# Nineteen gate and up pairs of a transformer layer made from seven block products each

## The chip, the core and the metric

The kernel runs on one core of a Trainium2 chip. TensorE (PE) multiplies, VectorE (DVE), ScalarE (ACT) and GpSimd (POOL) work on tiles, and DMAs are issued from the queues of SyncE (SP) and ScalarE. The metric is device time in microseconds of one execution. The kernel is float32: a product of two float32 matrices is made as three products of "high" and "low" parts (fp32r), and accumulated in PSUM.

## The reference

Two layers work on 512 latent and 256 context tokens of width 1024. What matters here is the second half of a layer, the gated feed-forward with a centred convolution of width 3 over the tokens:

```
def conv_ffn(h, w_up, conv_w, conv_b, w_down):
    u = h @ w_up                                  # 1024 -> 2 x 2816
    u = conv over tokens, width 3, per channel (u, conv_w) + conv_b
    a, bv = jnp.split(u, 2, axis=-1)
    return (jax.nn.silu(a) * bv) @ w_down
...
x = x + gt2 * conv_ffn(h2, ffn_up[l], ffn_conv_w[l], ffn_conv_b[l], ffn_down[l])
if with_ctx:
    ctx = ctx + cgt2 * conv_ffn(hc2, ...)
```

In layer 0 all 768 tokens go through it, in layer 1 only the 512 latent ones. The modulation vectors (`gt2` and others) are products of a conditioning vector with `ada_w`.

## The kernel before

Features lie on partitions, tokens in the columns. The normed input `h` is held as `hh` (high part) and `hl` (low part), eight blocks k of 128 features by 768 tokens. The 2816 hidden channels are 22 tiles of 128, and each tile has a gate half and an up half. One `Job` makes one half of one tile: it loads two raw weight tiles of 128x512 (`load`, on SP), splits each into `wh` (a copy by ACT, line 455) and `wl` (a subtraction, line 457, on DVE, on POOL for a few jobs), and multiplies in `chunk` (line 473): for every k three passes, hh with wh, hl with wh, hh with wl, over 512 and then 256 columns (`by_seg`). The result lies in a two-bank PSUM tile `pg`, of which there are two, so that job n+2 needs the bank of job n.

The evacuation `ev_up` makes the convolution: the centre tap by ACT (line 1484, scale and bias), the two side taps by DVE straight from PSUM (lines 1487, 1489), each for 512 and 256 columns. The gate half gets a SiLU (ACT, line 1496); after the up half the two are multiplied (DVE, line 1508) and split into `ah` (ACT) and `al` (DVE, line 576), the input of the down projection.

The 22 tiles come in groups (`GROUPS`) of 8, 7 and 7. After a group, eight down jobs multiply its 8 or 7 activation tiles with `dn` weights and add gate times result to `x` in SBUF (`residual`, line 1325, DVE).

The order is written out by program: `flow` walks through the list of jobs and issues for each, at fixed chunks, the loads and splits of the next two jobs and the evacuation of the last. Beside them run generators of side work: `beat` adds the nominal time of each matmul pass times `rate` to a budget, and a step of side work is issued for every unit of it. In the feed-forward of layer 0 the side work is `ada_rows`, the modulation vectors: per step a weight tile from DRAM and one or two DVE products with accumulation (line 656), with a small addition (line 659) in the second half. `rate` is 0.12 in the up jobs and 0.5 from the second down job on. Instructions of an engine run in the order in which they were issued.

## Time and profile before

| | |
|---|---|
| time, median of 3 runs | 2338.53 us (2338.52 to 2339.19) |
| the profiled execution: time, span | 2338.43 us, 2336.7 us |
| PE busy | 2296.9 us, 98% of the span, 13610 matmuls |
| DVE busy | 1417.8 us, 61% |
| ACT busy | 930.3 us, 40% |
| POOL busy | 299.9 us, 13% |
| chain that ended last | PE 86%, DVE 6%, ACT 3% |

"Busy" counts the time in which at least one instruction of the engine runs; matmuls overlap, so their mean length is larger than the time from one start to the next. The granted clock is a share of 2.4 GHz. The chain that ended last is followed back from the last instruction, at each step to what released it.

The feed-forward of layer 0 lies between about 822 and 1380 us: the first pair follows the norm chunk by chunk, and from 847.3 on jobs follow one another.

### The profile page before, as it was taken

Reading aid. Unit: us, or ns where it says so; the run is one execution under the profiler, and the core shown is the slowest. Engines: PE = TensorE matmul, PEld = TensorE weight load, DVE = VectorE, ACT = ScalarE, POOL = GpSimd, SP = SyncE. Lnnn points to the kernel's source line nnn. Section 1 sums busy time; section 2 is a strip of 40 time slices with the busy share of each in tenths; the row PEclk is TensorE's granted clock in tenths of the full one; section 3 lists DMA queues with packets and bytes.
Section 4 is the critical chain, followed back from the end, with each engine's and each line's share of the span. In section 5 each row is a group of like instructions: output and inputs, shape, how many; then the busy total and the mean of one; then the engine's idle time right before and its main releaser. Section 6 shows DMA issues by size and latency. Waiting matters only on the chain.

```text
span 2336.7 us, 35302 instructions
## 1 busy us (share of the span) xinstructions
PE 2296.9 (98%) x13610; PEld 1987.8 (85%) x13610; DVE 1417.8 (61%) x2856; ACT 930.3 (40%) x1623; POOL 299.9 (13%) x256
## 2 busy tenths in 40 slices
PE   8999999999999999999999999999999999999999
PEld 6888988888888888888888887989888888888887
DVE  5756485523878478766686656546753555646564
ACT  5655533322222253313313346554443335434342
POOL 0211163000111020000000024113500211000000
PEclk9999999999999999999999999999999999999999
DMA  7111112322454333462362322111233333332333
GB/s 269 50 41 39 53 51 95 94 65 88 144 169 137 104 100 108 136 185 95 103 195 91 104 86 69 46 46 51 95 114 116 95 108 105 99 99 92 99 99 100
DMA packets 132840, 235.79 MB, mean 101 GB/s; under 512 B 14460, under 2 KB 25980, under 8 KB 132544
## 3 DMA queue, kind: packets, MB, share of 16 engines
q1 hardware_dynamic: 123200, 223.57, 30.2%
q10 hardware_dynamic: 9472, 9.96, 1.2%
q8 instruction: 107, 1.75, 0.3%
q14 instruction: 61, 0.50, 0.1%
HBM read 220.37 MB, written 13.11 MB: 100 GB/s over the span
## 4 chain that ended last, share of the span: by engine, by line
PE 86%; DVE 6%; ACT 3%; issue 2%; POOL 1%; DMA 1%; POOLq 0%; ACTq 0%; SPq 0%; DVEq 0%
PE pg L473 72%; PE pg L485 6%; PE pm L912 2%; PE pm L901 1%; PE pm L1093 1%; PE ps L849 1%; PE pm L1115 1%; PE ps L848 1%; PE pm L1116 1%; DVE P L894 0%; DVE qs L1056 0%; PE pm L1282 0%; DVE Sg L1106 0%; DVE P L860 0%; DVE wl L457 0%
## 5 line engine op out<-in xcount | busy, mean ns | idle before, releaser
L473 PE MATMUL pg<-hh,wh 128*128 128x512 f32 (+1 forms) x2384 | 816.3, 354 | 7.4 <-ACT hh L1672 2.1
L473 PE MATMUL pg<-hl,wh 128*128 128x512 f32 (+1 forms) x2384 | 814.8, 354 | 0.8 <-POOL hl L307 0.7
L473 PE MATMUL pg<-hh,wl 128*128 128x512 f32 (+1 forms) x2384 | 812.5, 353 | 1.0 <-DVE wl L457 0.7
L457 DVE TENSOR_TENSOR wl<-raw,wh 128x512 fp32r<-128x512 f32 x500 | 356.5, 722 | 340.9 <-ACT wh L455 297.4
L473 PEld LDWEIGHTS pg<-hh,wh 128*128 128x128 f32 x2384 | 439.5, 190 | 72.8 <-issue 4.5
L473 PEld LDWEIGHTS pg<-hl,wh 128*128 128x128 f32 x2384 | 439.7, 190 | 61.3 <-DVE hl L1673 1.6
L473 PEld LDWEIGHTS pg<-hh,wl 128*128 128x128 f32 x2384 | 439.2, 189 | 61.0 <-issue 1.3
L455 ACT ACTIVATE wh<-raw 128x512 fp32r<-128x512 f32 (+1 forms) x556 | 334.4, 618 | 326.2 <-PE pg L473 163.2
L656 DVE SCALAR_TENSOR_TENSOR junk<-adr,crow 128x512 f32<-128x512 f32 x256 | 193.7, 757 | 11.2 <-DMA adr<-adv 7.5
L457 POOL TENSOR_TENSOR wl<-raw,wh 128x512 fp32r<-128x512 f32 x56 | 75.9, 1370 | 762.1 <-PE pg L473 549.7
L473 PE MATMUL pg<-al,wh 128*128 128x512 f32 (+1 forms) x500 | 171.5, 357 | 1.4 <-DVE al L576 1.4
L473 PE MATMUL pg<-ah,wh 128*128 128x512 f32 (+1 forms) x500 | 170.8, 356 | 0.0
L473 PE MATMUL pg<-ah,wl 128*128 128x512 f32 (+1 forms) x500 | 170.5, 355 | 0.0
L1313 POOL TENSOR_TENSOR M<-M,sg 128x768 f32<-128x768 f32 (+1 forms) x30 | 58.4, 1945 | 532.9 <-DVE sg L1311 532.9
L1301 ACT ACTIVATE sg<-pg 128x768 f32<-128x768 f32 (+1 forms) x48 | 33.7, 703 | 215.3 <-PE pg L473 215.3
L473 PEld LDWEIGHTS pg<-al,wh 128*128 128x128 f32 x500 | 91.4, 189 | 15.6 <-DVE al L576 2.3
L1487 DVE SCALAR_TENSOR_TENSOR acc<-pg,sml,acc 128x511 f32<-128x511 f32 (+1 forms) x129 | 84.8, 658 | 31.8 <-ACT acc L1484 31.4
L473 PEld LDWEIGHTS pg<-ah,wl 128*128 128x128 f32 x500 | 91.5, 189 | 13.8
L473 PEld LDWEIGHTS pg<-ah,wh 128*128 128x128 f32 x500 | 91.2, 189 | 13.9 <-ACT ah L575 0.4
L1325 DVE SCALAR_TENSOR_TENSOR X<-pg,mod,X 128x512 f32<-128x512 f32 (+1 forms) x72 | 45.7, 659 | 86.7 <-PE pg L473 86.7
L1484 ACT ACTIVATE acc<-pg,sml 128x768 f32<-128x768 f32 (+1 forms) x86 | 75.6, 879 | 38.2 <-PE pg L473 37.7
L1489 DVE SCALAR_TENSOR_TENSOR acc<-pg,sml,acc 128x511 f32<-128x511 f32 (+1 forms) x129 | 85.3, 661 | 4.6
(282 smaller groups left out, 3099.1 us busy)
## 6 DMA issues: line engine op xcount, KB each, us to landing
raw<-win SPq DMA_DIRECT2D x184, 256.0 KB, 2.9
raw<-up SPq DMA_DIRECT2D x176, 256.0 KB, 2.9
...
```

The costliest lines, as they stand in the source:

```text
L455: nc.scalar.activation(out=hi, in_=raw, func=AF.Copy)
L457: eng.tensor_tensor(out=lo, in0=raw, in1=hi.bitcast(F32), op=ALU.subtract)
L473: nc.tensor.matmul(job.ps[0:m, lo:hi], job.w[k // 4][a][:, k % 4, :], job.h(k, b)[:, lo:hi], start=(k == 0 and n == 0), stop=(k == job.nk ...
L485: nc.tensor.matmul(job.ps[:, 256 * t:256 * t + 256], job.h(k, b)[:, o:o + 128], job.w[k // 2][a][:, k % 2, :], start=(k == 0 and n == 0 an ...
L656: nc.vector.scalar_tensor_tensor(out=junk, in0=raw, scalar=1.0, in1=cr[v], op0=ALU.mult, op1=ALU.mult, accum_out=acc)
L912: nc.tensor.matmul(po[64 * kv:64 * kv + 64, 0:256], self.att["Va"][:, kb, 64 * kv:64 * kv + 64], PT[b][:, 256 * kv:256 * kv + 256], start= ...
L1301: nc.scalar.activation(out=sgs[d][:, 0:n], in_=ps[:, 0:n], func=AF.Tanh, scale=0.5)
L1313: eng.tensor_tensor(out=m, in0=m, in1=sg[:, 0:n], op=ALU.add)
L1325: nc.vector.scalar_tensor_tensor(out=X(d)[:, lo:hi], in0=ps[:, lo:hi], scalar=gate(d, int(lo >= TL)), in1=xin[:, lo:hi], op0=ALU.mult, op1 ...
L1484: nc.scalar.activation(out=acc[:, 0:nq], in_=ps[:, 0:nq], func=AF.Identity, scale=cw(1), bias=self.s("cb", 44 * l + u))
L1487: nc.vector.scalar_tensor_tensor(out=acc[:, lo + 1:hi], in0=ps[:, lo:hi - 1], scalar=cw(0), in1=acc[:, lo + 1:hi], op0=ALU.mult, op1=ALU.add)
L1489: nc.vector.scalar_tensor_tensor(out=acc[:, lo:hi - 1], in0=ps[:, lo + 1:hi], scalar=cw(2), in1=acc[:, lo:hi - 1], op0=ALU.mult, op1=ALU.add)
```

## The change

In layer 0 the first three tiles (`PLAIN`) stay as they are. The other 19 pairs go through the new class `Seven`. The weights of gate and up of a tile are a matrix of 2 x 2 blocks (gate or up, by features 0 to 511 or 512 to 1023: r11, r12, r21, r22), the input is one of 2 x 2 blocks (the same halves of the features, by tokens 0 to 383 or 384 to 767). Winograd's form of Strassen's scheme makes the product of the two from seven products of blocks, of 128 channels x 512 features x 384 tokens, with sums before and after.

- The sums of input blocks are made once (`blocks_begin`, `blocks_end`): 24 additions on POOL and 20 instructions on DVE of 384 columns, with splits, issued beside the plain tiles 1 and 2. They fill the tiles `T` (slots 1, 3 and 0), and one block `u` overwrites the right half of hh and hl, blocks 0 to 3.
- The sums of weight blocks are made for every pair on POOL (`weights`): four additions, and five of the seven low parts; the other two low parts are DVE's. There are three pairs of weight tiles, used in turn.
- The sums of products are made on DVE (`sums`), seven instructions of 384 columns from PSUM into SBUF tiles `g` and `u`. The taps then read those tiles. The stages 7 to 12 of a pair run beside the products of the next one, and after the last pair of a group in `tail`, beside the down jobs.
- Since slots 1 and 3 are taken, `x` is kept in DRAM (`xm`): the out projection stores it, each down job loads its tile (`xback`, two ahead) and stores it again (on ACT's queue), and only the last group's results stay in SBUF.
- The groups of layer 0 become 6, 6, 5 and 5 tiles. In the first two down jobs of a group the last chunk of the first comes after all but the last chunk of the second.
- The side work is paced anew: 0.04 in the pairs, 0.56 in the down jobs from the first on, and the products for `gt2` are put ahead, behind those of `sc2`.

```
-GROUPS = [(0, 8), (8, 15), (15, 22)]
+GROUPS = [[(0, 6), (6, 12), (12, 17), (17, 22)], [(0, 8), (8, 15), (15, 22)]]
+PLAIN = 3
+HT = TA // 2
...
+class Seven:
+    ORDER = ["p1", "p6", "p7", "p5", "p2", "p4", "p3"]
...
+    def parts(self, g, raw, eng):
...
+        hi, lo = self.q[g % 3]
+        p.split(self.r[raw], hi, lo, eng)
...
+    def weights(self, i, s):
...
+        if s == -3:
+            add("y", "r11", "r21")
+        elif s == -2:
+            self.parts(g, "r11", nc.vector)
+            add("x", "y", "r22")
+        elif s == -1:
+            self.parts(g + 1, "x", nc.gpsimd)
+        elif s == 0:
+            add("r21", "r21", "r22")
+            self.parts(g + 2, "y", nc.gpsimd)
+        elif s == 1:
+            self.parts(g + 3, "r21", nc.gpsimd)
+            add("x", "x", "r12")
+        elif s == 2:
+            self.parts(g + 4, "r12", nc.vector)
+        elif s == 3:
+            self.parts(g + 5, "r22", nc.gpsimd)
+        elif s == 4:
+            self.parts(g + 6, "x", nc.gpsimd)
...
+        if s == 1:
+            d["g"] = p.tP("g")
+            nc.scalar.activation(out=d["g"][:, left], in_=d["a"], func=AF.Copy)
+        elif s == 2:
+            d["V"] = p.t3("V")
+            tt(out=d["V"][:, left], in0=d["b"], in1=d["g"][:, left], op=V)
+        elif s == 3:
+            tt(out=d["V"][:, right], in0=d["c"], in1=d["V"][:, left], op=ALU.add)
...
+        elif s == 6:
+            tt(out=d["u"][:, left], in0=d["b"], in1=d["V"][:, right], op=ALU.add)
+            d["au"] = centre(d["u"], t + NFF)
+            tap(d["au"], d["u"], t + NFF, 0)
+        elif s == 7:
+            tt(out=d["g"][:, right], in0=d["c"], in1=d["g"][:, right], op=ALU.add)
+            d["ag"] = centre(d["g"], t)
+            tap(d["au"], d["u"], t + NFF, 2)
+        elif s == 8:
+            tap(d["ag"], d["g"], t, 0)
+        elif s == 10:
+            tap(d["ag"], d["g"], t, 2)
+            nc.scalar.activation(out=d["ag"], in_=d["ag"], func=AF.Silu)
+        elif s == 11:
+            tt(out=d["ag"], in0=d["ag"], in1=d["au"], op=ALU.mult)
+        elif s == 12:
+            self.end(t, d["ag"])
...
+            for s, name in enumerate(self.ORDER):
+                hi, lo = self.q[(7 * i + s) % 3]
+                T = self.blocks[name]
+                for m, (a, b) in enumerate(((hi, 0), (hi, 1), (lo, 0))):
+                    for k in range(4):
+                        nc.tensor.matmul(d[to[name]], a[:, 128 * k:128 * k + 128], T(k, b),
...
+                        self.sums(i - 1, s + 7)
+                        self.sums(i, s)
+                        self.weights(i, s)
+                        self.weights(i + 1, s - 7)
...
+    def tail(self, k):
+        for s in {0: (7,), 1: (8, 9), 2: (10, 11), 3: (12,)}.get(k, ()):
+            self.sums(len(self.pairs) - 1, s)
...
+            if seven:
...
+                for k in range(last):
+                    self.chunk(a, k)
...
+                    seven.tail(k)
...
+                for k in range(last):
+                    self.chunk(b, k)
...
+                self.chunk(a, last)
+                a.evac(a.ps)
+                self.split_w(n1)
+                self.chunk(b, last)
...
+        def dn_pre(g):
+            self.rate = 0.56
+            self.need("gt2")
...
+            xback(0, g)
+            xback(1, g)
```

Three places in the order of the instructions. First POOL, in the feed-forward of layer 0. Before, its row ends with the norm ahead of the first pair (`hl` from `room`), and the next instruction belongs to layer 1:

```order
L307 TENSOR_TENSOR hl<-room,hh 128x512
L457 TENSOR_TENSOR wl<-raw,wh 128x512 x2
L307 TENSOR_TENSOR hl<-room,hh 128x512 x2
L307 TENSOR_TENSOR hl<-room,hh 128x256 x4
L457 TENSOR_TENSOR wl<-raw,wh 128x512 x2
L307 TENSOR_TENSOR hl<-h,hh 128x512
```

Now, one pair of a run; L265 are the sums of weight blocks (`r_...` are the raw blocks r21, r22, r12), L784 the low parts:

```order
L265 TENSOR_TENSOR r_9554<-r_9554,r_9556 128x512
L784 TENSOR_TENSOR wl<-y,wh 128x512
L784 TENSOR_TENSOR wl<-r_9554,wh 128x512
L265 TENSOR_TENSOR x<-x,r_9557 128x512
L784 TENSOR_TENSOR wl<-r_9556,wh 128x512
L784 TENSOR_TENSOR wl<-x,wh 128x512
L265 TENSOR_TENSOR y<-r_9553,r_9554 128x512
L265 TENSOR_TENSOR x<-y,r_9556 128x512
L784 TENSOR_TENSOR wl<-x,wh 128x512
```

POOL goes from no instruction to nine in every pair. Second, DVE in the same place. Before, an up job and its neighbours (`pg` is PSUM, L1487 and L1489 the taps, L656 the modulation products, L576 the low part):

```order
L1487 SCALAR_TENSOR_TENSOR acc<-pg,sml,acc 128x511
L1489 SCALAR_TENSOR_TENSOR acc<-pg,sml,acc 128x511
L1487 SCALAR_TENSOR_TENSOR acc<-pg,sml,acc 128x255
L1489 SCALAR_TENSOR_TENSOR acc<-pg,sml,acc 128x255
L1508 TENSOR_TENSOR acc<-acc 128x768
L656 SCALAR_TENSOR_TENSOR junk,mod_108<-adr,crow 128x512 x2
L576 TENSOR_TENSOR al_8217<-acc,ah_8215 128x768
L457 TENSOR_TENSOR wl<-raw,wh 128x512 x2
```

Now, within a pair, from the sum in slot 6 on (`pg` and `ps` are PSUM, `g`, `u` and `V` SBUF; L303 are the taps, L341 the product, L865 a modulation product):

```order
L328 TENSOR_TENSOR u<-pg,V 128x384
L303 SCALAR_TENSOR_TENSOR acc<-u,sml,acc 128x511
L303 SCALAR_TENSOR_TENSOR acc<-u,sml,acc 128x255
L332 TENSOR_TENSOR g<-ps,g 128x384
L303 SCALAR_TENSOR_TENSOR acc<-u,sml,acc 128x511
...
L318 TENSOR_TENSOR V<-pg,g 128x384
L784 TENSOR_TENSOR wl<-r_9557,wh 128x512
...
L320 TENSOR_TENSOR V<-ps,V 128x384
L865 SCALAR_TENSOR_TENSOR junk,mod_109<-adr,crow 128x512
L341 TENSOR_TENSOR acc<-acc 128x768
```

The taps move from a PSUM operand to two SBUF operands, and the sums of products stand between them. Third, DVE at the end of group 0, from the last product of gate and up to the evacuation of the first down job. Before (L1325 is the evacuation):

```order
L1508 TENSOR_TENSOR acc<-acc 128x768
L457 TENSOR_TENSOR wl<-raw,wh 128x512
L576 TENSOR_TENSOR al_8217<-acc,ah_8215 128x768
L656 SCALAR_TENSOR_TENSOR junk,mod_108<-adr,crow 128x512 x2
L457 TENSOR_TENSOR wl<-raw,wh 128x512
L1325 SCALAR_TENSOR_TENSOR X_7379<-pg,mod_107,X_7379 128x512
```

Now (L1534 is the evacuation, into the loaded tile `xin`):

```order
L341 TENSOR_TENSOR acc<-acc 128x768
L865 SCALAR_TENSOR_TENSOR junk,mod_109<-adr,crow 128x512 x2
L784 TENSOR_TENSOR a_9017<-acc,a_9017 128x768
L626 TENSOR_TENSOR wl<-raw,wh 128x256
L865 SCALAR_TENSOR_TENSOR junk,mod_109<-adr,crow 128x512 x4
L626 TENSOR_TENSOR wl<-raw,wh 128x512
L865 SCALAR_TENSOR_TENSOR junk,mod_109<-adr,crow 128x512 x4
L1534 SCALAR_TENSOR_TENSOR xin<-pg,mod_108,xin 128x512
```

Between the product and the evacuation stand ten modulation products in place of two.

## Rows read from the trace of the kernel before

**Rows 1.** Stages: us, busy (instructions) of PE, PEld, DVE, ACT, POOL; clock, DMA.
```profile
847.30:963.80 116.50, 115.80 (x669) 102.23 (x668) 94.03 (x192) 44.67 (x65) 0.00 (x0) 1.00 0.36 114
963.80:1030.40 66.60, 66.60 (x384) 58.76 (x384) 51.03 (x122) 12.25 (x19) 0.00 (x0) 1.00 0.59 182
```

**Rows 2.** PE's waits, 848 to 1374 us: in all, times, longest.
```profile
PE pg L473 <- DVE al L576: 0.9, 1, 0.9
PE pg L473 <- DVE wl L457: 0.7, 1, 0.7
```

**Rows 3.** Timeline of PE in an up job: start, length, engine, line, operation.
```profile
902.27 0.39 PE L473 MATMUL pg<-hh,wl 128*128 128x512 f32 x1
902.50 0.28 PE L473 MATMUL pg<-hh,wh 128*128 128x256 f32 x1
902.61 0.28 PE L473 MATMUL pg<-hl,wh 128*128 128x256 f32 x1
```

**Rows 4.** Timeline, DVE beside POOL, both inputs in SBUF; in brackets idle before.
```profile
728.29 0.68 DVE L457 TENSOR_TENSOR wl<-raw,wh 128x512 fp32r<-128x512 f32 x1
728.89 2.33 DVE L656 SCALAR_TENSOR_TENSOR junk<-adr,crow 128x512 f32<-128x512 f32 x1
...
728.45 2.22 POOL L1313 TENSOR_TENSOR M<-M,sg 128x768 f32<-128x768 f32 x1 [10.30 <-DVE sg L1311]
...
1887.15 2.38 DVE L457 TENSOR_TENSOR wl<-raw,wh 128x512 fp32r<-128x512 f32 x2
...
1887.32 1.67 POOL L1313 TENSOR_TENSOR M<-M,sg 128x512 f32<-128x512 f32 x1 [6.49 <-DVE sg L1311]
```

**Rows 5.** Timeline, DVE with one operand in PSUM (ps) beside POOL.
```profile
308.90 1.11 POOL L1074 TENSOR_TENSOR sc<-Sg,E 128x512 f32<-128x512 f32 x1
...
309.14 0.69 DVE L1077 SCALAR_TENSOR_TENSOR at<-ps,con 128x512 f32<-128x512 f32 x1
```

**Rows 6.** POOL undisturbed: timeline, three in a row; then a group (busy, mean ns).
```profile
1406.81 3.77 POOL L457 TENSOR_TENSOR wl<-raw,wh 128x512 fp32r<-128x512 f32 x3 [3.36 <-ACT wh L455]
...
L307 POOL TENSOR_TENSOR hl<-room,hh 128x256 fp32r<-128x256 f32 x12 | 9.0, 754 | 61.4 <-ACT room L292 61.4
```

**Rows 7.** Timeline of DVE at the end of group 0.
```profile
967.46 0.96 DVE L1508 TENSOR_TENSOR acc<-acc 128x768 f32<-128x768 f32 x1
...
969.34 0.96 DVE L576 TENSOR_TENSOR al<-acc,ah 128x768 fp32r<-128x768 f32 x1 [0.31 <-ACT ah L575]
970.21 0.68 DVE L656 SCALAR_TENSOR_TENSOR junk<-adr,crow 128x512 f32<-128x512 f32 x1
...
970.94 0.69 DVE L656 SCALAR_TENSOR_TENSOR junk<-adr,crow 128x512 f32<-128x512 f32 x1
...
972.44 1.14 DVE L1325 SCALAR_TENSOR_TENSOR X<-pg,mod,X 128x512 f32<-128x512 f32 x2 [0.20 <-PE pg L473]
```

**Rows 8.** Groups by shape, 847.3 to 1380 us: busy us, mean ns, idle before.
```profile
L1496 ACT ACTIVATE acc<-acc 128x768 f32<-128x768 f32 x22 | 18.6, 847 | 56.5 <-DVE acc L1489 56.3
...
L659 DVE SCALAR_TENSOR_TENSOR mod<-mod,sml,aacc 128x1 f32<-128x1 f32 x80 | 17.6, 220 | 2.9
...
L457 DVE TENSOR_TENSOR wl<-raw,wh 128x384 fp32r<-128x384 f32 x14 | 7.7, 552 | 3.0 <-ACT wh L455 3.0
...
L1489 DVE SCALAR_TENSOR_TENSOR acc<-u,sml,acc 128x511 f32<-128x511 f32 x1 | 0.8, 751 | 0.0
...
L1489 DVE SCALAR_TENSOR_TENSOR acc<-u,sml,acc 128x255 f32<-128x255 f32 x1 | 0.5, 484 | 0.0
```

**Rows 9.** PE after a wait: timeline; then two stretches as in rows 1.
```profile
827.00 1.44 PE L252 MATMUL pm<-con,sq 128*128 128x2 f32 x6 [2.77 <-ACT sq L239]
...
832.71 0.63 PE L473 MATMUL pg<-hh,wl 128*128 128x512 f32 x1
...
828.00:830.00 2.00, 2.00 (x7) 1.71 (x7) 1.18 (x3) 1.95 (x3) 1.27 (x1) 0.50 0.00 0
1384.00:1388.00 4.00, 2.78 (x17) 2.30 (x16) 3.52 (x5) 2.86 (x6) 3.69 (x3) 1.00 0.25 98
```

More of the change, by code (lines that the diff above doesn't have):

```diff
@@ L433, in split_w @@
     def split_w(self, job, part=1):
-        if job is None:
+        if job is None or isinstance(job, Seven):
             return
@@ L631, in ada_rows @@
         nc = self.nc
-        self.rate = rate
+        if rate is not None:
+            self.rate = rate
         junk = self.t2("junk")
@@ L1398, in fill0 @@
             if l == 0:
[L1399 removed]
+                for a, b, tag, rate in ((16, 24, "gt1", 0.5), (24, 40, "sc2", 0.3), (40, 48, "gt2", 0.3)):
                     self.side.append(self.tagged(tag, self.ada_rows(0, [(t, 2) for t in range(a, b)], rate)))
@@ L1457, in f @@
                         nm.square(d, 1.6)
+                if l == 0:
+                    lo, hi = sg[0][0], sg[-1][1]
+                    nc.scalar.dma_start(out=self.xm[:, d, lo:hi], in_=self.X(d)[:, lo:hi])
             return f
@@ L1553, in layer_jobs, with end @@
                 jobs += J[2:]
+                if not last:
+                    J[2].pre = lambda: self.blocks_begin(o)
             else:
                 jobs += J
-            if g:
+            if not last:
+                def end(t, a, t0=t0):
+                    if t == t0:
+                        new_act()
+                    self.split(a, o["act_at"](t - t0, 0), o["act_at"](t - t0, 1))
+                jobs.append(Seven(self, lambda u: self.i["up"][0, u], list(range(max(t0, PLAIN), t1)), self.blocks(o), end))
+                if g == 0:
+                    jobs[-1].pre = lambda: self.blocks_end(o)
+            elif g:
                 J[2].pre = lambda: setattr(self, "rate", 0.12)
@@ L1559, in layer_jobs @@
             src = lambda d, t0=t0, t1=t1: self.i["dn"][l, d, :, t0 * 128:t1 * 128]
-            if g == len(GROUPS) - 1 and not last:
+            if g == len(groups) - 1 and not last:
                 homes = {d: lambda t=t: (t[:, :, 512:640], t[:, :, 640:768]) for d, t in ((4, self.hh), (5, self.hl))}
-                jobs += self.ordered(order, lambda n, g=g: ev_dn(order[n][0], g, order[n][1]), src, act, ng, homes)
+                J = self.ordered(order, lambda n, g=g: ev_dn(n, order[n][0], g, order[n][1]), src, act, ng, homes)
@@ L1564, in layer_jobs @@
             else:
-                jobs += [Job(src(d), act, cols, ev_dn(d, g, cols), nk=ng) for d in range(8)]
-                for j in jobs[-7:]:
+                J = [Job(src(d), act, cols, ev_dn(d, d, g, cols), nk=ng) for d in range(8)]
+                for j in J[1:]:
                     j.by_seg = True
-                jobs[-7].pre = lambda: setattr(self, "rate", 0.5)
-        return jobs
+            if last:
+                J[1].pre = lambda: setattr(self, "rate", 0.5)
+                jobs += J
+                continue
@@ new lines, in layer_jobs, with blocks @@
+            J[0].pre = lambda g=g: dn_pre(g)
+            jobs.append((J[0], J[1], None))
+            jobs += J[2:]
+            if g < len(groups) - 1:
+                J[7].pre = lambda: setattr(self, "rate", 0.04)
+        return jobs
+    def blocks(self, o):
+        h = lambda k0, lo: lambda k, part: self.h(k0 + k, part)[:, lo:lo + HT]
+        t = lambda n: lambda k, part: o["T"][n][:, part, k, :]
+        return dict(p1=h(0, 0), p2=h(4, 0), p3=h(4, HT), p7=h(0, HT), p5=t(0), p6=t(1), p4=t(2))
@@ new lines, in blocks_begin, with gen, step @@
+    def blocks_begin(self, o):
+        nc = self.nc
+        o["T"] = T = [self.slot(k, [128, 2, 4, HT], F32R, name=f"T{k}") for k in (1, 3, 0)]
+        o["w"] = w = self.slot(5, [128, 8, HT], name="w")
+        def gen():
+            for k in range(4):
+                b = [self.h(k, p)[:, lo:lo + HT].bitcast(F32) for p in range(2) for lo in (0, HT)]
+                c = [self.h(k + 4, p)[:, lo:lo + HT].bitcast(F32) for p in range(2) for lo in (0, HT)]
+                t1, t2, t4 = (t[:, 1, k, :] for t in T)
+                f1, f2, f4 = (w[:, n, :] for n in (4, 5, 6))
+                u = w[:, k, :]
+                op = lambda e, out, a, b, f: e.tensor_tensor(out=out, in0=a, in1=b, op=f)
+                S, P = nc.vector, nc.gpsimd
+                op(S, f1, b[0], b[2], ALU.add)
+                op(P, u, b[1], b[3], ALU.add)
+                yield
+                op(S, f2, c[1], c[3], ALU.add)
+                op(P, f4, c[0], c[2], ALU.add)
+                yield
+                op(P, f1, f1, u, ALU.subtract)
+                yield
+                op(S, u, u, f2, ALU.subtract)
+                op(P, f2, f2, f1, ALU.add)
+                yield
+                op(P, f4, f4, f2, ALU.subtract)
+                nc.scalar.activation(out=T[0][:, 0, k, :], in_=f1, func=AF.Copy)
+                op(S, t1, f1, T[0][:, 0, k, :].bitcast(F32), ALU.subtract)
+                yield
+                for n, f, t, e in ((1, f2, t2, S), (2, f4, t4, P)):
+                    nc.scalar.activation(out=T[n][:, 0, k, :], in_=f, func=AF.Copy)
+                    op(e, t, f, T[n][:, 0, k, :].bitcast(F32), ALU.subtract)
+                yield
+        o["gen"] = g = gen()
+        def step():
+            if next(g, self) is not self:
+                self.defer(1.2, step)
+        self.defer(1.2, step)
@@ L1571, in ordered, with blocks_end @@
+    def blocks_end(self, o):
+        for _ in o["gen"]:
+            pass
+        for k in range(4):
+            self.split(o["w"][:, k, :], self.hh[:, k, HT:TA], self.hl[:, k, HT:TA], self.nc.gpsimd if k % 2 else None)
     def ordered(self, order, evac, src, h, nk, homes):
@@ L1590, in run @@
         self.xd1 = self.dp.tile([128, 8, TA], F32, name="xd1")
+        self.xm = self.dp.tile([128, 8, TA], F32, name="xm")
         self.Xs = [self.slot(k, [128, 4, TA], name=f"X{k}") for k in (1, 3)]
```

174 lines of the change are left out of this document (153 added, 21 removed).

## The prediction, made before the changed kernel ran

> **What bounds the kernel now.** I read the table by stages first. In the feed-forward of layer 0 TensorE (PE) is busy 115.80 us of 116.50 in the seven up pairs behind the first one and 66.60 of 66.60 in the eight down jobs after them, at a granted clock of 1.00, that is 2.4 GHz [rows 1]. The waits of PE over the whole stage come next: 0.9 us on the low part of an activation and 0.7 us on the low part of a weight, nothing else [rows 2]. So a matmul taken out here is time taken out, as long as nothing else grows longer than PE's new time. VectorE (DVE) stands at 94.03 and 51.03 us in these stretches, GpSimd (POOL) at zero [rows 1]: the reader should see one engine full, one half full, one free. The change hands the free one most of its new work.
>
> **What PE saves.** A stretch of seven pairs takes 116.5 us, 16.64 us a pair [rows 1]: 48 matmuls of 512 columns, which follow each other at 0.23 us, and 48 of 256 at 0.11 to 0.12 us [rows 3]. One of 384 columns lies halfway in columns, so I give it the mean, 16.64 / 96 = 0.1733 us. The new pair has 84 of them: 14.56 us, 2.08 less. Over 19 pairs that is 39.5 us, if PE alone sets the pace.
>
> **What the pair adds: turns at one input.** In the rows, DVE and POOL do not run side by side when DVE reads two tiles from SBUF. At 728.89 a DVE instruction that takes 0.68 us alone takes 2.33, while POOL's addition of 768 columns runs until 730.67; it ends 0.55 us after POOL does. At 1887.15 two splits of 0.68 us take 2.38 together, and POOL's addition of 512 columns, which starts between them, ends 1.16 us after the first of them [rows 4]. One turn of POOL is thus 1.16 us, one of DVE with 512 columns 0.54 to 0.57. DVE with one operand in PSUM is not held: 0.69 us beside a running POOL instruction [rows 5]. Before the change none of this meets in the feed-forward, since POOL is idle.
>
> A new pair has nine POOL instructions of 512 columns: 9 x 1.16 = 10.4 us. Of DVE's, the taps now read a tile in SBUF instead of PSUM, so they take turns too: eight instructions, four of 511 and four of 255. Their lengths are 0.75 and 0.48 us [rows 8]; in a turn, less the part in which neighbours overlap, 0.60 and 0.37, so 3.9 us. Two weight splits cost 1.1, the product and the low part of 768 columns (0.96 each, [rows 7]) 1.7. The seven additions from PSUM take no turn. Sum 10.4 + 3.9 + 1.1 + 1.7 = 17.1 us. One gap stays in which neither can go: the SiLU (0.85 us, [rows 8], with hand-overs 0.95) stands between the last taps and the product, and ScalarE's next weight copy, which POOL needs, is queued behind it. So a pair in full swing costs 18.1 us, more than PE's 14.56 and more than the old 16.64.
>
> On this the Trainium skill speaks (SBUF — State Buffer, "Who interferes with whom"): a VectorE instruction with two SBUF inputs and a GpSimd instruction that reads SBUF exclude each other, and the later one blocks completely until the first ends. Taken to the letter, with whole lengths, the sum would be higher; that is the third rival. The rows agree with the exclusion, and show that neighbours hand over some 0.1 us early.
>
> Not every pair is in full swing. The first pair of each of the four runs has no sums of a pair before it; its turns (10.4 + three splits 1.7 + two taps 1.0) stay under PE's time: 14.56 us. In the second the queues fall behind, but three pairs of weight tiles and the four banks carry PE: I give it 14.9. The other eleven pay 18.1. Together 4 x (14.56 + 14.9) + 11 x 18.1 = 316.9 us, against 19 x 16.64 = 316.2: **+0.7**. The whole gain is eaten. About ten modulation products (two SBUF inputs) still stand between the pairs in DVE's new order, 0.6 us each: **+6**. Bounds for the pair: 17.0 (no gap, early hand-overs) and 20.5.
>
> **The sums of the blocks** run beside two plain pairs (33.3 us) and 3.5 us more, until the second product's last third needs them. They are 24 POOL instructions of 384 columns, between the 0.75 us of 256 columns and the 3.77 / 3 = 1.26 of 512 [rows 6], 0.9 in a turn: 21.6; 20 of DVE (0.55 alone [rows 8], 0.45 in a turn): 9; beside them seven weight splits 4.0, products and low parts 3.5, four modulation products 2.4, the first two weight sums and a split 3.5, the u block's parts 2.7. That is 46.7 us of turns for 36.8. Some 2 us are needed later: **+8**, between 3 and 13.
>
> **The ends of the four groups.** Here the order of DVE is the term. Before, the last up job's taps, product, split and low part are followed within 2 us by the evacuation of the first down job, and PE waits 0.9 us once [rows 2, 7]. After, the third down job needs the bank of the first, whose evacuation stands behind the seven products' last sums and behind modulation products at the new rate. One of these costs 0.73 us from start to start [rows 7], 0.86 where the small instruction (0.22, [rows 8]) follows. In group 0, from the last tap of the up half: two products 1.7, the right sum 0.5, taps 1.0, two products 1.5, taps 1.0, split 0.6, taps 1.0, SiLU and product 1.85, two products 1.5, low part 0.9, split 0.4, four products 2.9, split 0.6, four products 2.9, evacuation 1.1: 19.5 us. DVE begins this some 2.2 us after PE's last product (an estimate: the left sum of the up half, ScalarE's centre tap and two taps stand in between): 21.7. PE has only twelve chunks to fill that, at 66.6 / 64 = 1.04 us [rows 1]: 12.5. It waits 9.2 us. The same count gives 16.9 against 12.5 in group 1, and, with ten chunks, 19.8 and 15.6 against 10.4 in groups 2 and 3: 4.4, 9.4, 5.2. Sum **+28**; without the 2.2 us of lag 19, with 1.5 us more of it 34. These waits replace the one of 0.9 of before: **-1**. In the later jobs of group 2 DVE has 6.6 us a job (five modulation products of 0.86, evacuation 1.14, splits 0.8, less what falls late) for PE's 5.2, until the two-sided rows end: **+2**, 0 to 6.
>
> **The clock.** After PE stood for 2.77 us at 827.00 the rows show 0.50 of the clock, 1.2 GHz, and matmuls of 512 columns 0.63 us long (0.39 otherwise, [rows 3]) until 833; at half the clock for 6 us, some 3 us are lost. After shorter gaps (2.78 us of 4 busy at 1384) it stayed at 1.00 [rows 9]. The four ends have waits of 6.3, 3.3, 5.4 and 3.0 us before the third down job; half of what a slow PE then loses is hidden, since DVE is late there anyway: **+6**, 0 to 16.
>
> **At nothing:** x through DRAM (two tiles are fetched ahead; ScalarE's store is issued after an evacuation and waits for nothing else; a down job is 5.2 us or more, which covers the fetch; without that cover about 3 us a job), the second gate's products moved ahead of the feed-forward (DVE has room beside the branches; else 1 to 2 us), and the down matmuls, equal in number.
>
> **Sum.** The profiled execution took 2338.43 us, like the median 2338.53. 0.7 + 6 + 8 + 28 - 1 + 2 + 6 = +49.7: **2388 us**. With all lower bounds (pairs -11, products 4, 3, 19, -1, 0, 0) 2352.
>
> **Rivals.** (1) *PE keeps the pace.* It holds if a tap and a POOL instruction pass freely; then DVE's and POOL's 10 to 11.5 us a pair fit in 14.56. The pairs give -39.5, the block sums 0, the ends 19 (no lag), the rest 4: 2322. It decides from the point where a pair's turns drop under 14.56. For it: DVE beside POOL with one PSUM operand [rows 5]. Against: both overlaps in [rows 4]. (2) *The buffers carry further:* the third pair of each run is also 14.9, the others 17.0, all else at the lower bounds: pairs -20, so 2338.4 - 20 + 4 + 3 + 19 - 1 = 2344. For it: a wait here decides only when three products are used up. Against: the lag grows by some 3 us a pair. (3) *Whole lengths:* 9 x 1.26 + 2 x 0.69 + 4 x 1.23 + 2 x 0.96 + 0.95 = 20.5 us a pair, 26 more over eleven, the block sums 3 more: 2417. Against: both hand-overs in [rows 4] are shorter. By the Trainium skill's rule this is the one that comes; the trace bears it out in kind, not in length.
>
> **How the numbers follow.** Forecast 0.66, rival (1) 0.11, (2) 0.09, (3) 0.14. About 0.2% (4.7 us) is what a measurement of this kernel can tell from no change. Faster is (1): 0.11. Same is about half of (2) and the rim of the forecast: 0.06. Slower: 0.83. The range leaves out (1), most of (2) below and a small rest above: 2347 to 2420.
>
> **What would show it.** In the changed profile, POOL's instructions of 512 columns in the pairs read 1.6 to 2 us instead of 1.26, and DVE's two-input ones often over 1.5; PE is busy about 80% of the later pairs of a run and near 100% of the first; its waits name the low weight parts of POOL and DVE and ScalarE's copies; before the third down job of each group stands a wait of 3 to 6 us on an evacuation, with a granted clock under 1 behind it. The forecast is wrong if taps of 0.6 us lie inside POOL instructions of 1.26, or if the third down job starts without a wait.

## The result, and the profile of the changed kernel

The changed kernel takes 2510.6 us (median of four, 2507.5 to 2511.9) against 2338.9 us (2338.5 to 2340.3): a ratio of 1.073, 95% interval 1.071 to 1.075. It is slower, as forecast, by 172 us where 50 were forecast, and far outside the range of 2347 to 2420. The profiled execution took 2509.6 us with a span of 2507.8.

The table by stages (columns as in [rows 1]) cuts the feed-forward of layer 0 at the first matmul of each part: the two plain pairs with the sums of the blocks; then pairs and down stage of the four groups in turn; last the first 15 us of layer 1.

```profile
847.30:890.57 43.27, 35.33 (x202) 30.48 (x201) 36.77 (x54) 18.50 (x28) 22.85 (x20) 1.00 0.18 55
890.57:961.66 71.09, 50.92 (x252) 47.52 (x253) 50.59 (x66) 26.57 (x43) 44.65 (x32) 0.88 0.19 59
961.66:1028.28 66.62, 55.16 (x289) 46.51 (x289) 49.96 (x125) 11.24 (x21) 0.51 (x1) 0.95 0.68 219
1028.28:1148.58 120.30, 100.63 (x506) 94.62 (x505) 82.25 (x112) 45.82 (x70) 78.85 (x54) 0.93 0.24 74
1148.58:1205.68 57.10, 52.98 (x289) 45.33 (x289) 36.53 (x85) 10.09 (x19) 1.47 (x1) 0.97 0.73 246
1205.68:1309.97 104.29, 84.00 (x422) 79.17 (x421) 71.62 (x105) 38.93 (x60) 64.68 (x44) 0.92 0.23 73
1309.97:1370.39 60.42, 47.92 (x242) 39.87 (x241) 46.78 (x137) 9.18 (x18) 0.00 (x0) 0.92 0.64 209
1370.39:1476.50 106.11, 86.80 (x421) 81.41 (x422) 69.88 (x97) 37.87 (x58) 64.62 (x45) 0.89 0.22 72
1476.50:1542.49 65.99, 50.38 (x261) 41.50 (x261) 49.27 (x126) 19.59 (x39) 2.81 (x2) 0.92 0.59 195
1542.49:1557.49 15.00, 11.81 (x35) 9.08 (x35) 7.18 (x11) 8.20 (x15) 5.91 (x5) 0.55 0.25 87
```

Against [rows 1], where PE is all but full in both stages: the 19 pairs take 71.09 + 120.30 + 104.29 + 106.11 = 401.8 us, 21.1 each, where 19 x 16.64 = 316.2 stood: **+85.6**. The four down stages take 250.1 us. Before, three took 66.6 [rows 1] and, in the same view of the kernel before, 58.3 and 64.5, the last with the start of layer 1's norm; 189.4 together: **+60.7**. The plain pairs take 43.3 for 33.3: **+10**. Layer 1, from its first matmul on, takes 965.3 us where it took 950.5: **+14.8**. Together 171.1, the difference of the spans.

```profile
1146.90:1205.20 58.30, 57.38 (x327) 50.22 (x326) 53.84 (x159) 11.93 (x20) 0.00 (x0) 1.00 0.59 183
1321.70:1386.24 64.54, 63.32 (x376) 55.92 (x375) 35.02 (x65) 21.79 (x40) 3.64 (x3) 1.00 0.33 104
```

The waits of PE from 890 to 1477 us, longest sums first, stand beside two waits of under 1 us in [rows 2]:

```profile
PE pg L363 <- ACT g L315: 48.7, 19, 9.9
PE pg L642 <- DVE xin L1534: 18.3, 8, 5.1
PE ps L363 <- DVE V L320: 15.1, 19, 2.0
PE pg L363 <- DVE g L326: 14.2, 19, 1.5
```

Three of the four come once in every one of the 19 pairs, 78 us in all, and the prediction's sum has none of them. Of the 19 on L315, the first, eleven take 2.0 us, three 0.6, and five from 2.7 to 9.9. The timeline shows one in group 1 (bracket: the idle time ahead and what ended it):

```profile
1083.03 1.50 PE L363 MATMUL pg<-T,wh 128*128 128x384 f32 x7 [0.65 <-DVE g L326]
...
1089.23 0.34 PE L363 MATMUL pg<-T,wh 128*128 128x384 f32 x1
...
1089.61 1.03 ACT L308 ACTIVATE acc<-g,sml 128x768 f32<-128x768 f32 x1 [2.19 <-DVE g L332]
1090.54 0.61 ACT L783 ACTIVATE wh<-y 128x512 fp32r<-128x512 f32 x1
1091.06 0.47 ACT L315 ACTIVATE g<-pg 128x384 f32<-128x384 f32 x1
...
1091.58 2.36 PE L363 MATMUL pg<-T,wh 128*128 128x384 f32 x7 [2.01 <-ACT g L315]
```

The first matmul of p6, into half b of the tile `pg`, starts at 1089.23. Its second waits 2.01 us for ScalarE's copy of half *a* of the same tile (L315). That copy reads nothing that p6 writes. It is issued behind p6's first matmul, and the dependency is kept for the whole tile of two banks; so PE, in the middle of a product, waits for ScalarE, which has just finished a centre tap and a weight copy for others. The listing of PE's instructions shows it without a time: p6 begins with two matmuls that wait on ScalarE, and p5 and p4 have a second matmul that waits on VectorE.

```
L363 MATMUL pg_11489<-T3_8289,wh_10943 128x384 [waits Activation_49] x2
...
L363 MATMUL ps_10936<-T1_8288,wh_10929 128x384 [waits Activation_49]
L363 MATMUL ps_10936<-T1_8288,wh_10929 128x384 [waits DVE_49]
...
L363 MATMUL pg_11489<-T0_8290,wh_10907 128x384 [waits Activation_49]
L363 MATMUL pg_11489<-T0_8290,wh_10907 128x384 [waits DVE_49]
```

The wait also costs clock. The seven matmuls behind it take 2.36 us; those of p4 in the pair before, at 1083.03 after a wait of 0.65, take 1.50. Two stretches, right behind this wait and a little later:

```profile
1091.58:1095.68 4.10, 4.10 (x15) 4.10 (x15) 2.03 (x3) 1.10 (x2) 4.06 (x3) 0.58 0.08 12
1095.68:1097.50 1.82, 1.82 (x11) 1.57 (x10) 1.82 (x5) 0.00 (x0) 0.00 (x0) 1.00 0.75 260
```

A wait of 2.0 us was enough for 4 us at a granted clock of 0.58, mostly at 1.2 GHz. It was not so each time: of the eleven waits of 2.0 us on this copy ten have such a stretch behind them (0.58 to 0.62), and this one, in group 0, has none; the next 4.1 us stand at 1.00:

```profile
946.31 1.51 PE L363 MATMUL pg<-T,wh 128*128 128x384 f32 x7 [2.02 <-ACT g L315]
```

In the pairs, 19 x 14.56 = 276.6 us of matmuls and 78 of these waits leave 47 of 401.8. The table's clock of 0.88 to 0.93 withholds at most 37 of them (0.12 x 71.09 + 0.07 x 120.30 + 0.08 x 104.29 + 0.11 x 106.11). Most of the rest is a matter of counting: a wait is counted from the end of the matmul before it, which lasts 0.34 us, while at full pace the next one starts 0.17 us after that one's start; 57 waits x 0.17 = 10 us.

The forecast's turns are there too: POOL's 512 columns take 1.98 us here, 1.26 undisturbed in [rows 6], and VectorE's 768 columns 1.35 instead of the 0.96 of [rows 7].

```profile
1081.10 1.35 DVE L784 TENSOR_TENSOR a<-acc,a 128x768 fp32r<-128x768 f32 x1
...
1081.60 1.98 POOL L265 TENSOR_TENSOR y<-r,r 128x512 f32<-128x512 f32 x1
```

### The profile page after: what moved, and what is told of

It is laid out like the page before. It is cut to its first block, busy times and chain, and to the rows that moved or that the text cites. A ratio compares the mean times of both kernels' runs of the same rounds, so it can differ in the third digit from the quotient of the medians.

```text
span 2507.8 us, 35763 instructions
## 1 busy us (share of the span) xinstructions
PE 2333.3 (93%) x13382; PEld 2024.7 (81%) x13382; DVE 1546.6 (62%) x3005; ACT 981.3 (39%) x1731; POOL 578.9 (23%) x453
## 5 line engine op out<-in xcount | busy, mean ns | idle before, releaser
L642 PE MATMUL pg<-hh,wh 128*128 128x512 f32 (+1 forms) x1776 | 613.6, 361 | 15.4 <-DVE X L1534 6.7
L642 PE MATMUL pg<-hl,wh 128*128 128x512 f32 (+1 forms) x1776 | 611.7, 360 | 4.2 <-POOL hl L476 4.0
L642 PE MATMUL pg<-hh,wl 128*128 128x512 f32 (+1 forms) x1776 | 609.7, 359 | 1.0 <-DVE wl L626 0.7
L626 DVE TENSOR_TENSOR wl<-raw,wh 128x512 fp32r<-128x512 f32 (+3 forms) x440 | 310.2, 714 | 311.8 <-ACT wh L624 291.1
L624 ACT ACTIVATE wh<-raw 128x512 fp32r<-128x512 f32 x496 | 289.4, 604 | 270.2 <-DVE xin L1534 62.3
L642 PEld LDWEIGHTS pg<-hh,wh 128*128 128x128 f32 x1776 | 324.7, 190 | 69.2 <-issue 8.1
L642 PEld LDWEIGHTS pg<-hl,wh 128*128 128x128 f32 x1776 | 324.7, 190 | 55.0 <-POOL hl L476 5.6
L642 PE MATMUL pg<-a,wh 128*128 128x512 f32 (+1 forms) x1016 | 276.9, 367 | 31.0 <-DVE xin L1534 18.3
L642 PEld LDWEIGHTS pg<-a,wh 128*128 128x128 f32 x1016 | 182.1, 195 | 66.3 <-issue 23.1
L865 DVE SCALAR_TENSOR_TENSOR junk<-adr,crow 128x512 f32<-128x512 f32 x256 | 199.3, 778 | 22.3 <-DMA adr<-adv 18.2
L1522 POOL TENSOR_TENSOR M<-M,sg 128x768 f32<-128x768 f32 (+1 forms) x30 | 58.3, 1944 | 535.5 <-DVE sg L1520 535.5
L642 PE MATMUL pg<-a,wl 128*128 128x512 f32 (+1 forms) x508 | 176.9, 365 | 3.1 <-DVE wl L626 2.9
L363 PE MATMUL pg<-T,wh 128*128 128x384 f32 x304 | 85.0, 412 | 64.3 <-ACT g L315 48.7
L642 PEld LDWEIGHTS pg<-a,wl 128*128 128x128 f32 x508 | 94.9, 194 | 20.5 <-DVE wl L626 6.2
L303 DVE SCALAR_TENSOR_TENSOR acc<-u,sml,acc 128x511 f32<-128x511 f32 x76 | 66.0, 909 | 20.9 <-ACT acc L308 20.9
L265 POOL TENSOR_TENSOR y<-r,r 128x512 f32<-128x512 f32 x19 | 32.7, 1724 | 198.5 <-DMA r<-up 126.9
L1080 ACT ACTIVATE P<-P,st,rq 128x512 f32<-128x512 f32 (+2 forms) x80 | 64.8, 810 | 20.2 <-DVE st L1072 16.3
```

Of the source, the lines that this page charges most:

```text
L265: add = lambda out, a, b: nc.gpsimd.tensor_tensor(out=r[out], in0=r[a], in1=r[b], op=ALU.add)
L303: nc.vector.scalar_tensor_tensor(out=acc[:, o[0]:o[1]], in0=raw[:, x[0]:x[1]], scalar=cw(u, j), in1=acc[:, o[0]:o[1]], op0=ALU.mult, op1=A ...
L363: nc.tensor.matmul(d[to[name]], a[:, 128 * k:128 * k + 128], T(k, b), start=(m == 0 and k == 0), stop=(m == 2 and k == 3))
L624: nc.scalar.activation(out=hi, in_=raw, func=AF.Copy)
L626: eng.tensor_tensor(out=lo, in0=raw, in1=hi.bitcast(F32), op=ALU.subtract)
L642: nc.tensor.matmul(job.ps[0:m, lo:hi], job.w[k // 4][a][:, k % 4, :], job.h(k, b)[:, lo:hi], start=(k == 0 and n == 0), stop=(k == job.nk ...
```

## Experiments

The kernel before took 2338.9 to 2340.5 us on the chips used. Each version here was run once; the four runs of the changed kernel lie 4.4 us apart, so a difference of a few us between two versions shows little.

### Successive products in different tiles

```diff
-        banks = dict(c=ps[:, 0:HT], d=ps[:, 512:512 + HT])
+        banks = dict(b=ps[:, 0:HT], d=ps[:, 512:512 + HT])
-            d.update(banks, a=pg[:, 0:HT], b=pg[:, 512:512 + HT])
+            d.update(banks, a=pg[:, 0:HT], c=pg[:, 512:512 + HT])
```

> Edit: the same seven products and the same sums, but successive products write to different PSUM tiles: the two halves of the tile pg take p1, p7, p2 and p3, those of ps take p6, p5 and p4. Theory A (a wait on the whole PSUM tile): in the changed kernel the second matmul of p6, p5 and p4 waits for a sum that reads the other half of the same tile; 78 us of TensorE waits in the 19 pairs, and the clock that they cost. With it the three waits all but vanish from the pairs (under 15 us in all) and a pair takes 15 to 17.5 us in place of 21.1: 2425 to 2445 us or less. Theory B (turns of VectorE and GpSimd at a shared SBUF input, the step of the prediction): other waits take their place, a pair stays at 18.1 us or more: 2450 us or more.

Measured: 2465.6 us, 45 less than the changed kernel; pairs 360.9 us (65.8, 107.6, 94.4, 93.1), 19.0 each; down stages 249.0, about as in the changed kernel. So the waits on the whole tile were real and cost 41 us of the pairs with their clock, and what remains is in the range that theory B gave. Theory A was right about the waits, theory B about the time that is left; whether it is the turns that fill it, the next two experiments test. Of PE's waits, ScalarE's copy falls from 48.7 to 14.8, and another comes up:

```profile
PE ps L363 <- DVE V L318: 16.1, 8, 3.5
PE pg L363 <- ACT g L315: 14.8, 6, 5.8
```

How a turn becomes such a wait is seen at 1061 us of this version:

```profile
1061.00 1.47 POOL L784 TENSOR_TENSOR wl<-y,wh 128x512 fp32r<-128x512 f32 x1
...
1061.24 3.19 DVE L303 SCALAR_TENSOR_TENSOR acc<-g,sml,acc 128x511 f32<-128x511 f32 x2
...
1062.42 1.73 POOL L784 TENSOR_TENSOR wl<-r,wh 128x512 fp32r<-128x512 f32 x1
...
1064.35 0.55 DVE L318 TENSOR_TENSOR V<-ps,g 128x384 f32<-128x384 f32 x1
...
1065.05 2.80 PE L363 MATMUL ps<-T,wh 128*128 128x384 f32 x8 [1.55 <-DVE V L318]
```

Two taps (511 and 255 columns, 1.14 us alone) take 3.19 between POOL's weight parts; the sum behind them in VectorE's queue is late; PE waits 1.55 us for it and then runs eight matmuls in 2.80 us instead of 1.55.

### Taps that read PSUM

```diff
-            tt(out=d["g"][:, left], in0=d["a"], in1=d["g"][:, left], op=ALU.add)
+            tt(out=d["a"], in0=d["a"], in1=d["g"][:, left], op=ALU.add)
...
-            d["ag"] = centre(d["g"], t)
+            d["ag"] = centre(d["graw"], t)
```

(`graw` is the tile `pg` from column 128 to 896, with a and c side by side in it; the second kernel does the same with b, d and `ps`.)

> Edit, on top of the other tiles for successive products: the last two sums of the gate are written back into its PSUM tile, and ScalarE's centre tap and VectorE's four other taps of the gate read it there in place of SBUF. The products and sums are the same. Theory B (the pair is now bound by VectorE and GpSimd taking turns at SBUF, some 18 us of turns): four of VectorE's taps leave the turns, about 2.3 us a pair, and the pairs go from 19.0 to about 17 us: 2420 to 2440 us. Rival G (a chain through the engines' queues sets the pair, and not the turns): within 10 us of 2465.

> Edit, on top of the one before: the up half is kept in PSUM too, in its single tile ps, so that all eight of VectorE's taps read PSUM. Theory B: the turns fall to about 13.7 us and TensorE's 14.56 us would set the pair; but p6 of the next pair must wait until the taps of this pair's up half are done. 2385 to 2420 us if that wait is under 1 us a pair. Rival G (a chain through queues): the wait at p6 takes 2 to 4 us a pair, and the time is 2430 to 2480 us.

Measured: 2440.3 us with the gate in PSUM, pairs 335.7; 2435.4 us with both, pairs 325.1. The gate alone ends a hair above theory B's range, at 17.7 us a pair, and 15 below rival G's. From start to start of the same sum (line 318), pairs inside a run take mostly 18.1 to 19.7 us with other tiles alone, mostly 16.2 to 17.3 with the gate in PSUM, and with both 15.1 to 15.5 in half of them, within a microsecond of PE's 14.56; the others, with waits, take up to 19.8. Grouped by shape, the taps of the pairs of group 1, with other tiles alone and then with both halves in PSUM:

```profile
L303 DVE SCALAR_TENSOR_TENSOR acc<-g,sml,acc 128x511 f32<-128x511 f32 x10 | 12.6, 1258 | 0.0
...
L303 DVE SCALAR_TENSOR_TENSOR acc<-g,sml,acc 128x255 f32<-128x255 f32 x10 | 9.8, 983 | 0.0
```

```profile
L303 DVE SCALAR_TENSOR_TENSOR acc<-pg,sml,acc 128x511 f32<-128x511 f32 x10 | 7.4, 744 | 0.1
...
L303 DVE SCALAR_TENSOR_TENSOR acc<-pg,sml,acc 128x255 f32<-128x255 f32 x10 | 4.7, 471 | 0.0
```

The same taps, beside the same POOL instructions, take 744 and 471 ns from PSUM and 1258 and 983 from SBUF. A rival would be that a tap from SBUF is slower by itself. The version of the next section, where POOL does nothing in the pairs, settles it; there the taps from SBUF take 744 and 477 ns:

```profile
L303 DVE SCALAR_TENSOR_TENSOR acc<-g,sml,acc 128x511 f32<-128x511 f32 x10 | 7.4, 744 | 0.0
...
L303 DVE SCALAR_TENSOR_TENSOR acc<-g,sml,acc 128x255 f32<-128x255 f32 x10 | 4.8, 477 | 0.0
```

So the difference is the turn, priced directly: half a microsecond a tap. The Trainium skill (SBUF — State Buffer, "Who interferes with whom") says that an instruction of VectorE with at most one SBUF input, outside its two-port modes, does not contend with GpSimd; these rows agree. The second half gained 10.6 us in the pairs and 5 in the whole: ahead of the first pair the plain pairs took 4 us longer, layer 1 took 2 more. The next pair's p6 has to wait until the taps have left `ps`, 0.9 us a pair on average; that is within theory B's condition, yet the time lies in rival G's range, so neither theory fits whole.

```profile
PE ps L362 <- DVE acc L303: 16.8, 15, 3.6
```

### GpSimd's part on VectorE

```diff
-        add = lambda out, a, b: nc.gpsimd.tensor_tensor(out=r[out], in0=r[a], in1=r[b], op=ALU.add)
+        add = lambda out, a, b: nc.vector.tensor_tensor(out=r[out], in0=r[a], in1=r[b], op=ALU.add)
...
-            self.parts(g + 1, "x", nc.gpsimd)
+            self.parts(g + 1, "x", nc.vector)
```

(and the four other calls of `parts` likewise)

> Edit, on top of the other tiles for successive products: GpSimd's nine operations of a pair on the weights (four sums of blocks, five lower halves) go to VectorE; GpSimd does nothing in the pairs. Theory B (turns): VectorE runs at its undisturbed lengths, about 16.5 us of work a pair, and a pair takes 16.5 to 17.5 us in place of 19.0: 2420 to 2440 us. Rival G (a chain through VectorE's queue sets the pair): the chain gets longer by operations that stand ahead of the sums, a pair takes 19 to 21 us: 2465 to 2505 us.

Measured: 2458.0 us, 7.6 less than with GpSimd at work; pairs 354.5, inside a run mostly 18.2 us. Neither expectation was met. One pair:

```profile
1085.00:1103.20 18.20, 15.63 (x84) 14.38 (x84) 16.07 (x29) 7.76 (x12) 0.00 (x0) 1.00 0.20 59
```

VectorE works 16.07 us at undisturbed lengths, about the 16.5 expected, and stands still for 2.13: 1.10 on ScalarE's centre tap and 1.03 on a weight copy, which its one queue can't fill. So turns are not all that keeps a pair above 14.56 us: without any, VectorE's own work and two waits give 18.2. And GpSimd's help, at its price in turns, was worth nothing in this version, or a little less.

### The rest of the change without the seven products

```diff
-PLAIN = 3
+PLAIN = 22
```

> Edit: all 22 pairs are made plainly (eight products); the groups of 6, 6, 5 and 5, x in DRAM and the rates of the background rows stay as in the changed kernel. It prices what the change does beside the seven products. The changed kernel's four down stages take 250 us where 183 us of matmuls stand in them, and layer 1 begins with 15 us more than before. Theory C (these costs come from x in DRAM and from the rates): they stay, 2400 to 2420 us. Theory D (they follow from the seven products: the sums of the last pair, the clock after their waits): the down stages go back to about 195 us, 2345 to 2365 us.

> Edit, on the kernel with 22 plain pairs, groups of 6, 6, 5 and 5 and x in DRAM: the background rows (modulation of layer 1) run at a rate of 0.33 in the pairs and 0.05 in the down stages, in place of 0.04 and 0.56. Theory C1 (the down stages are longer because the rows that the change moves there keep VectorE and the DMA queues from the residuals): the down stages fall from 221 to 190 to 200 us, 2350 to 2362 us. Theory C2 (the loads and stores of x cost that by themselves): the down stages stay over 210 us, 2372 to 2390 us.

Measured: 2384.4 us with the changed kernel's rates and 2365.4 with rates turned round. In the first the pairs cost what they cost before (100.1 us for six), the down stages 220.7, between the two theories; in the second the down stages are 197.3, as theory C1 has them, and the time 3 us above its range. Two of them:

```profile
937.84:989.05 51.21, 50.70 (x291) 44.25 (x290) 23.49 (x44) 9.54 (x18) 0.00 (x0) 1.00 0.60 190
...
1089.13:1141.83 52.70, 50.70 (x291) 44.25 (x290) 29.47 (x67) 9.80 (x19) 0.00 (x0) 1.00 0.62 199
```

Six column blocks of matmuls are 6 x 66.6 / 8 = 49.95 us by [rows 1]. With every x fetched and stored, these down stages cost 1.3 and 2.7 us more than their matmuls, once few background rows stand there. Of the 31 us by which the plain kernel's down stages exceed those of before, 23 are the rows' place; x in DRAM and the fourth group together are left with 8 at most. The other 19 us by which this kernel is slower than the one before lie in the first pairs, where rows now stand (7.5), and in layer 1 (11.1).

### The background rows

The changed kernel with its rates turned round (0.33 in the pairs, 0.05 in the down stages), and the version with both halves in PSUM at even rates and with the rates turned round:

```diff
-            self.rate = 0.56
+            self.rate = 0.05
...
-                self.rate = 0.04
+                self.rate = 0.33
```

> Edit, on the changed kernel: only the rates of the background rows, 0.33 in the pairs and 0.05 in the down stages, in place of 0.04 and 0.56; everything else as in it. The plain version of this edit took 23 us from the four down stages and 19 us from the time. Theory H (the down stages suffer from the rows whatever the pairs are): the down stages fall from 250 to about 225 us; the rows then stand in pairs whose VectorE, ScalarE and GpSimd form the bound, at about 0.9 us for one in turn with GpSimd, 4 to 5 rows a pair, and take the gain back: 2505 to 2525 us. Rival I (the waits of the pairs leave VectorE enough time for the rows): 2475 to 2495 us.

> Edit, on the version with both halves kept in PSUM (2435 us, down stages 249 us, pairs 325 us): the background rows run at 0.2 in pairs and down stages alike. Theory H: the down stages fall to 215 to 225 us, the pairs grow by 0.5 to 1 us each (VectorE has some 22 us free in the 93 us of the second run of pairs), 2405 to 2425 us. Rival J (the down stages are long because the sums of the last pair stand ahead of the first residual, whatever the rows): they stay over 235 us, 2430 to 2450 us.

> Edit, on the version with both halves kept in PSUM: rates of 0.33 in the pairs and 0.05 in the down stages. Theory H: the down stages fall to 205 to 215 us, the pairs grow by 1 to 2 us each: 2400 to 2425 us. Rival J: the down stages stay over 225 us: 2440 to 2460 us.

Measured: 2525.6 us, down stages 196 (50.6, 50.9, 43.9, 50.2), pairs 466.5. In the PSUM version 2449.4 at even rates (down stages 219, pairs 367) and 2457.9 turned round (203 and 391), against 2435.4 as it was (249 and 325). Theory H was right about the down stages and wrong about the price in the pairs: all three lose more there than they win. The last two times lie in rival J's ranges, but not for its reason, since the down stages are short. A down stage and the pairs behind it in the first of the three:

```profile
986.98:1037.55 50.57, 50.28 (x290) 44.20 (x290) 25.22 (x49) 10.76 (x20) 2.59 (x2) 1.00 0.62 195
1037.55:1175.17 137.62, 103.97 (x507) 98.21 (x506) 110.47 (x166) 46.50 (x72) 78.80 (x52) 0.90 0.32 103
```

> Edit, on the changed kernel: the background rows of layer 1 are loaded and multiplied on 16 of their 512 columns only (so the modulation of layer 1 leaves out most of its sum); their number, order and rates stay. Theory K (the rows are what lengthens the down stages): these fall from 250 to 195 to 205 us, layer 1 starts some 10 us faster, 2440 to 2460 us. Rival J (the ends of the groups and x in DRAM do it): the down stages stay over 225 us, 2475 to 2505 us.

> The same edit (rows on 16 of 512 columns) on the version with both halves kept in PSUM (2435 us, down stages 249 us, pairs 325 us). Theory K: down stages 195 to 205 us, pairs 310 to 320 us, 2360 to 2380 us. Rival J: down stages over 225 us, 2395 to 2425 us.

> The same edit (rows on 16 of 512 columns) on the kernel before. Theory K needs the rows to be nearly free there, since TensorE waits little and VectorE is 45 to 77% busy in its pairs and down stages: 2330 to 2339 us. If the rows cost there what they cost in the changed kernel, 2280 to 2300 us.

```diff
+                    cut = 512 if l == 0 else 16
-                    nc.sync.dma_start(out=raw, in_=self.i["adv"][l, hf, jobs[n][0]])
+                    nc.sync.dma_start(out=raw[:, 0:cut], in_=self.i["adv"][l, hf, jobs[n][0]][:, 0:cut])
```

(and the product on the same columns)

Measured: 2339.6 us in the kernel before, where the rows are thus free; 2466.9 in the changed kernel, 44 less; 2390.1 in the PSUM version, 45 less. The down stages, 217.3 and 216.9, and both times lie above theory K's ranges and below its rival's: 33 us of the down stages are the rows' own work, 10 of the 44 lie in the pairs. In the last 217, some 20 us more than with few rows there, the short rows keep their number and their place in the queues; that this is the cause was not separated.

### Stores of x from another queue

```diff
-                        nc.scalar.dma_start(out=self.xm[:, d, :], in_=x)
+                        nc.gpsimd.dma_start(out=self.xm[:, d, :], in_=x)
```

> Edit: the stores of x to DRAM in the first three down stages go out from GpSimd's queue in place of ScalarE's; nothing else. Theory E (ScalarE stands still behind a store whose residual VectorE has not made, and the weights of the next job wait for ScalarE): the waits of down jobs on ScalarE's halves of the weights (7.4 us) go, with the clock behind them: 2490 to 2500 us. Rival F (the residual is late, because VectorE makes background rows ahead of it, and TensorE waits for its PSUM tile whoever stores): 2505 to 2512 us.

> Edit: both of the two edits before, other tiles for successive products, and stores of x from GpSimd's queue. Theories A and E together: the sum of both gains, 2405 to 2435 us. If the pairs are bound by the turns at the SBUF input and the stores cost nothing: 2445 to 2460 us.

Measured: 2510.1 us, no change: rival F. On top of the other tiles 2474.4, which is 9 us slower than those alone and above both ranges; why was not followed up. ScalarE's long idle spells behind the store cost nothing, since the residual is late in VectorE's queue. In the changed kernel's first down stage:

```profile
980.32 0.69 DVE L865 SCALAR_TENSOR_TENSOR junk<-adr,crow 128x512 f32<-128x512 f32 x1
...
981.05 0.69 DVE L865 SCALAR_TENSOR_TENSOR junk<-adr,crow 128x512 f32<-128x512 f32 x1
...
981.67 1.14 DVE L1534 SCALAR_TENSOR_TENSOR xin<-pg,mod,xin 128x512 f32<-128x512 f32 x2
...
982.96 1.19 PE L642 MATMUL pg<-a,wh 128*128 128x512 f32 x2 [4.77 <-DVE xin L1534]
```

No version beats the kernel before. The best with seven products that computes everything takes 2435.4 us; even with the rows nearly free it is 2390.1.

## Why the prediction was wrong

- *PE's saving, right.* A 384-column matmul follows the next at 0.17 us, and with other tiles the first pair of group 1, which has no waits, takes 14.57 us for 14.56.
- *Turns at one input, right in kind and nearly in size.* 18.1 us forecast; mostly 18.1 to 19.7 measured once the false waits are gone, and down to 15.1 when the taps read PSUM. The size is partly luck: with GpSimd idle and no turn at all a pair took 18.2 too. What shows the turns is the length of the taps and the 25 us that the gate's taps gave back. The changed kernel's 20.2 to 20.9 us in group 1 look like rival (3), whole lengths, 20.5. They are not: the version with other tiles has the same instructions.
- *A step that was missing: waits on a whole PSUM tile.* The prediction followed the four banks as four buffers ("the four banks carry PE"). The program keeps order by the tile of two banks. The listing of the changed kernel's PE, with its waits, shows two waiting matmuls at the head of p6, p5 and p4; the prediction counted what engines do and not what PE's instructions wait for. Price: 41 us.
- *"Not every pair is in full swing", right for three of the first pairs, wrong for the second ones.* The first pair of each run was given 14.56 us, the second 14.9, since "three pairs of weight tiles and the four banks carry PE". With other tiles, from PE's first matmul of a pair to that of the next, the first pairs of the four runs take 27.12, 14.57, 15.16 and 16.86 us, the second ones 21.46, 17.20, 20.63 and 18.82, and the other eleven 19.0 each. In group 1:

```profile
1024.62:1039.19 14.57, 14.57 (x87) 14.57 (x85) 6.61 (x11) 5.98 (x10) 11.81 (x10) 1.00 0.35 115
1039.19:1056.39 17.20, 15.55 (x86) 14.37 (x85) 16.10 (x22) 7.51 (x12) 13.31 (x9) 1.00 0.19 61
```

  Against the forecast that is 15.5 us for the first pairs (12.6 of it in group 0), 18.5 for the second and 10.0 for the rest, less the 6 counted for modulation products: 38. 401.8 - (316.9 + 6) = 79 is the miss on the pairs, 41 of false waits and these 38.
- *The clock, mis-sized.* 6 us, up to 16, were forecast for four long waits. The rows chosen ([rows 9]) had 2.77 us with a fall and shorter gaps without. In the pairs, where no clock was counted, it costs up to 37 us behind waits of mostly 2.0 us, nearly all of it inside the 79 above.
- *The ends of the groups, wrong in mechanism.* 28 - 1 + 2 = 29 forecast, 60.7 measured. The waits ahead of the third down job are 4.8, 1.7, 5.1 and 2.5 us, less than the 9.2, 4.4, 9.4 and 5.2 in the forecast's sum (its paragraph on the clock has 6.3, 3.3, 5.4 and 3.0 for the same waits, which does not fit that sum); the loss goes through all the down jobs. The forecast put the rows into its sum at the first two jobs only and gave the rest 2 us. With few rows there the stages fall to 196 us.
- *The sums of the blocks, right in size, in part by luck:* 8 forecast, between 3 and 13; 10 measured up to the first of the seven products. But PE waits there 4.2 us for that product's weight copy and 3.0 for taps of the plain pairs, and not for a block that is needed later; the sums run on beside the first pair of group 0. *x through DRAM at nothing, right* within 8 us, by the plain kernel with few rows in the down stages (197.3 against 189.4).
- *Not in the sum: layer 1.* At its start PE stands 6.45 us where it stood 1.22 before, then 3.18 more, and runs at a clock of 0.55 for 15 us. Some 8 of the 14.8 us are lost in the first 28; the rest comes later in the layer, and its cause is open. The seven products are not needed for most of it: the plain kernel with the same groups takes 12.4 us more than before in layer 1, and 11.1 with few rows in the down stages, where the norm makes PE wait only 1.0 and 1.8 us. That five column blocks in the last group cover the norm's start less well than seven did is likely, but was not tested by itself. Before, then in the changed kernel:

```profile
1386.24 0.47 PE L473 MATMUL pg<-hh,wh 128*128 128x512 f32 x1 [1.22 <-DVE X L1325]
...
1542.49 0.77 PE L642 MATMUL pg<-hh,wh 128*128 128x512 f32 x1 [6.45 <-DVE X L1534]
...
1547.72 0.79 PE L642 MATMUL pg<-hl,wh 128*128 128x512 f32 x1 [3.18 <-POOL hl L476]
```

From 49.7 us to 171.1: pairs 78.9 more, down stages 31.7, layer 1 14.8, block sums 2, less the 6 us that were counted for the clock by itself. Of the range's bounds, the pair's upper one (20.5) would nearly have held inside group 1; no bound stood for the clock inside the pairs, for the rows in the later down jobs, or for layer 1.
